# Two gate projections as stages of seven block products, attention on two tracks, and the first branch's values in blocks of 512 columns

## The chip, the core and the metric

One core of a Trainium2 chip runs the whole program. Its engines work side by side and wait for each other through semaphores: TensorE (PE in the profile, its weight loads PEld) multiplies matrices into PSUM, VectorE (DVE) and ScalarE (ACT) do elementwise work, GpSimd (POOL) does some adds and issues DMAs, and SyncE (SP) issues most loads. The metric is device time in microseconds (us) of one execution; a comparison uses the median of several.

## The reference

One layer of a decoder trunk on x (1024 x 1024, float32). One combined projection feeds two mixers that run in parallel on the same input: HGRN2 (8 heads of 128) and gated linear attention (GLA, 4 heads with 128 key and 256 value columns). Each has a SiLU gate z, each is projected, and sigmoid gates merge them:

```python
proj = h @ w_in[l]                                   # h: modulated RMS norm of x
hq, hf, hi, hz, gq, gk, gv, gz, ga, mg = jnp.split(proj, IN_OFFSETS, axis=-1)
y_h = rms_norm(linear_attention(silu(hq), k, hi, log_f, 1.0), hgrn_norm_w) * silu(hz)
y_g = rms_norm(linear_attention(gq, gk, gv, log_a, K ** -0.5), gla_norm_w) * silu(gz)
u_h, u_g = y_h @ w_branch[l, 0], y_g @ w_branch[l, 1]
mg = sigmoid(mg.reshape(B, T, 2, D))
merged = mg[:, :, 0] * u_h + mg[:, :, 1] * u_g
x = x + gate[:, None, :] * (merged @ w_out[l])
return rms_norm(x, final_norm_w)
```

The HGRN norm goes over all 1024 columns, the GLA norm over one head's 256. The attention is computed by chunks of 64 steps.

## The kernel before

Every float32 product is made of three matmuls on operands split in a high and a low part (`split`, L195 for the low part on DVE): high times high, high times low, low times high. Activations lie transposed, channels on partitions, 1024 steps along the free side.

The program has four parts. **The beginning** loads x, makes the modulation and the transposed normalised input `h_hi`, `h_lo`, and the first projections. **The stream** (`Stream.go`) runs a list of jobs: `Feat` projects 128 columns (48 matmuls of 512 columns, L454), `Vblk` makes one GLA head's 256 value columns (192 matmuls of 256 columns, L513 to L515), `Vblk2` makes 512 value columns for four HGRN heads (192 matmuls of 512 columns, L556 to L558). After every unit of a job (six matmuls of 512 columns, or twelve of 256) `weave` lets two tracks advance by a count of units: `side`, the attention of one head after another, and `back`, which prepares factors and weights for the last part. **The stages** (`last_stages`, `Pair.run`, L1313) are large products in a block form with seven products of half size in place of eight (`PRODUCTS`): a stage has 7 products x 4 pairs of column blocks x 12 matmuls = 336. Before, there are four: the two merge gates from h (stages 0 and 1, sharing the factors `H` of h), and the two branch projections (2 and 3). Their factors are sums of quadrants of the activations; their weights are raw quadrants or sums of quadrants. The sums of weights are made early by `weight_sums` (two loads, four adds on DVE, four stores to `w_sums` in DRAM) and fetched again by `load_duo`; `prep_duo` splits them (L1256), `build` splits the factors (L1234). **The end** (`OutBlk`) is the output projection and the last norm.

`attention` (L570 on) has a first half that builds a head's masked scores in `scT` with many small DVE steps, and a second half that makes the states and the outputs and calls `post`. `post` multiplies the output by the norm weight and by the gate, which `silu_done` (L865, L866) had made from a z projection; the result is stored to `yg_d` or `yh_d`. Only one attention runs at a time on `side`. The last one reaches into stage 0: `scores_done` and `side_done` wait for it there before its PSUM banks are lent to the stages. The norm of the HGRN branch, `rst_h`, is known when its last head is done, and `scale_quad` (L1212) applies it when stage 3's quadrants have been loaded.

The order in which an engine's instructions stand is set by a scheduler from these calls and a planner's costs; each engine then runs strictly in that order, and so does the queue of loads on SP. Tiles of 4 KB per partition come from 46 slots (`Slots`), and `ahead` loads and splits weights while enough of them are free.

Of the kernel before, what the change touches and what calls it, by code (L numbers as in the profile page):

```python
# [15 lines left out]
P = 128  # L16
# [66 lines left out]
def hybrid_trunk_kernel(  # L83
# [346 lines left out]
    scoring = set()  # L430
# [48 lines left out]
    class Vblk:  # L479

        raws, parts = 2, 4

        def __init__(self, col, done):
            self.col, self.done = col, done

        def load(self):
            self.raw = []
            for kk in range(2):
                b = S.get([4, 256])
                nc.sync.dma_start(b, w_in2[kk * 512:(kk + 1) * 512, self.col:self.col + 256].rearrange(  # L490
                    "(k p) f -> p k f", p=P))
                self.raw.append(b)

        def prep(self):
            self.wt = []
            for b in self.raw:
                hi = S.get([4, 256], F32R)
                lo = S.get([4, 256], F32R)
                split(b, hi, lo)
                self.wt.append((hi, lo))  # L500
                S.free(b)

        def run(self):
            v = [S.get([4, 256]) for _ in range(2)]
            for g in range(2):
                ps = dtile()
                for i in range(4):
                    t = g * 4 + i
                    for k in range(KT):
                        hi, lo = self.wt[k // 4]  # L510
                        lh, ll = h_hi[k][:, t * P:(t + 1) * P], h_lo[k][:, t * P:(t + 1) * P]
                        o = ps[:, i * 256:(i + 1) * 256]
                        nc.tensor.matmul(o, lh, hi[:, k % 4, :], start=(k == 0), stop=False)  # L513
                        nc.tensor.matmul(o, lh, lo[:, k % 4, :], start=False, stop=False)  # L514
                        nc.tensor.matmul(o, ll, hi[:, k % 4, :], start=False, stop=(k == KT - 1))  # L515
                        if k % 4 == 3:
                            yield
                nc.scalar.copy(v[g].rearrange("p a b -> p (a b)"), ps)
            for hi, lo in self.wt:
                S.free(hi, lo)  # L520
            self.done(v)

    class Vblk2:

        raws, parts = 4, 8
# [18 lines left out]
        def run(self):  # L544
            v = [S.get([2, 512]) for _ in range(4)]
            for g in range(4):
                if g == 2:
                    self.middle()
# [992 lines left out]
```

## Time and profile before

| what | value |
|---|---|
| median of 3 runs | 1251.07 us (1250.69 to 1251.1) |
| the profiled execution | 1252.38 us |
| its span, first to last instruction | 1250.7 us |
| granted PE clock, mean | 0.99 |
| stream (L454 first and last start) | 127.9 to 825.3 us |
| stages (L1313 first and last start) | 825.5 to 1154.0 us |
| last weight sum stored (L1171) | 606.9 us |

A row of the groups by line reads: line, engine, operation, output and inputs, shape, count, then busy us and mean ns of one, then how long the engine stood idle before such an instruction and what ended it. Busy time counts stretches in which two instructions overlap once. A row by stretches reads: start and end, length, then busy us and count for PE, PEld, DVE, ACT and POOL, then granted clock, DMA share and GB/s.

### The profile page before, as it was taken

The page shows a single profiled execution, that of the slowest core. Times are in us where ns is not written, and L with a number is a line of the kernel's source. Part 1 is how long each engine was busy: PE and PEld are TensorE (multiplying, and loading weights), DVE is VectorE, ACT ScalarE, POOL GpSimd, SP SyncE. Part 2 cuts the span into 40 slices and gives each one's busy share as a digit, 9 for nine tenths or more (in the row PEclk, how much of TensorE's full clock was granted, in tenths as well). Part 3 has the DMA queues.
Part 4 walks back from the last instruction along what each step waited for, and adds up shares of the span by engine and source line. Part 5 has one row for each costly group of instructions (what it writes and reads, how often), then busy time and mean ns, then how long its engine had stood idle before and what let it go on. Part 6 is the DMA issues. An engine that isn't in the chain of part 4 may idle for free.

```text
span 1250.7 us, 20782 instructions
## 1 busy us (share of the span) xinstructions
PE 1205.7 (96%) x8603; PEld 999.9 (80%) x8603; DVE 765.2 (61%) x1219; ACT 530.4 (42%) x784; POOL 132.4 (11%) x216
## 2 busy tenths in 40 slices
PE   4799999999999999999999999999999999998997
PEld 3676899989798888788887878877888888787786
DVE  5746425494857556777873365695422668979443
ACT  4467713343334344243332323456643644454222
POOL 5510000201211021021110101011110000000000
PEclk9899999999999999999999999999999999999999
DMA  8832100653644167255251212154546556235202
GB/s 269 278 115 86 52 18 18 217 188 102 203 143 144 63 208 254 92 179 174 96 177 45 60 41 68 38 183 169 173 163 225 179 171 201 83 100 170 118 34 101
DMA packets 126928, 168.82 MB, mean 135 GB/s; under 512 B 7019, under 2 KB 97185, under 8 KB 126834
## 3 DMA queue, kind: packets, MB, share of 16 engines
q1 hardware_dynamic: 115234, 129.53, 33.5%
q0 software_dynamic: 11552, 37.97, 7.8%
q8 instruction: 67, 1.10, 0.4%
q14 instruction: 27, 0.22, 0.1%
q10 hardware_dynamic: 48, 0.01, 0.0%
HBM read 125.53 MB, written 41.94 MB: 134 GB/s over the span
## 4 chain that ended last, share of the span: by engine, by line
PE 59%; issue 24%; DVE 8%; DMA 3%; POOL 2%; ACT 2%; SPq 1%; POOLq 0%; DVEq 0%; ACTq 0%
PE pd L454 13%; PE pd L1313 11%; PE sc_ps L1313 5%; PE pm L1313 5%; PE pd L556 2%; PE pd L557 2%; PE pd L558 2%; DVE scT L250 1%; PE pm L761 1%; PE pm L742 1%; PE pm L763 1%; PE pd L1083 1%; PE pd L1084 1%; PE pd L1085 1%; DVE b L195 1%
## 5 line engine op out<-in xcount | busy, mean ns | idle before, releaser
L454 PE MATMUL pd<-b,b 128*128 128x512 f32 x1632 | 386.3, 393 | 0.0
L454 PEld LDWEIGHTS pd<-b,b 128*128 128x128 f32 x1632 | 302.4, 188 | 64.0 <-issue 0.5
L1313 PE MATMUL pd<-b,b 128*128 128x512 f32 x720 | 175.7, 395 | 2.5 <-DVE b L866 1.5
L1313 PEld LDWEIGHTS pd<-b,b 128*128 128x128 f32 x720 | 134.7, 189 | 35.4 <-DVE b L866 1.9
L195 DVE TENSOR_TENSOR b<-b,b 128x1024 fp32r<-128x1024 f32 (+1 forms) x95 | 101.8, 1082 | 74.7 <-ACT b L192 34.8
L192 ACT CAST b<-b 128x1024 fp32r<-128x1024 f32 (+1 forms) x95 | 84.6, 904 | 104.0 <-DVE b L1169 14.7
L1256 DVE TENSOR_TENSOR b<-b,b 128x1024 fp32r<-128x1024 f32 x56 | 68.3, 1224 | 68.5 <-ACT b L1255 46.6
L1255 ACT CAST b<-b 128x1024 fp32r<-128x1024 f32 x56 | 58.5, 1051 | 62.8 <-PE pd L1313 17.2
L1313 PE MATMUL sc_ps<-b,b 128*128 128x512 f32 x324 | 79.0, 391 | 0.3 <-ACT scT L706 0.3
L1313 PE MATMUL pm<-b,b 128*128 128x512 f32 x300 | 72.5, 389 | 3.4 <-DVE b L1256 3.4
L513 PE MATMUL pd<-b,b 128*128 128x256 f32 x256 | 74.2, 290 | 0.0
L515 PE MATMUL pd<-b,b 128*128 128x256 f32 x256 | 72.5, 283 | 0.0
L514 PE MATMUL pd<-b,b 128*128 128x256 f32 x256 | 72.4, 283 | 0.0
L1313 PEld LDWEIGHTS sc_ps<-b,b 128*128 128x128 f32 x324 | 60.4, 188 | 13.6 <-ACT scT L706 0.8
L1313 PEld LDWEIGHTS pm<-b,b 128*128 128x128 f32 x300 | 56.3, 188 | 15.5 <-DVE b L1256 3.8
L1234 DVE TENSOR_TENSOR b<-b,b 128x1024 fp32r<-128x1024 f32 x36 | 45.1, 1263 | 18.1 <-ACT b L1233 10.3
L1171 POOL DMA_DIRECT2D ws<-b x64 | 34.6, 541 | 194.8 <-DVE b L1165 87.1
L556 PE MATMUL pd<-b,b 128*128 128x512 f32 x128 | 52.0, 406 | 0.0
L557 PE MATMUL pd<-b,b 128*128 128x512 f32 x128 | 50.4, 394 | 0.0
L558 PE MATMUL pd<-b,b 128*128 128x512 f32 x128 | 50.4, 394 | 0.0
L648 ACT COPY xb<-b 128x512 f32<-128x512 f32 x48 | 29.5, 620 | 49.3 <-PE sc_ps L628 26.3
L1233 ACT CAST b<-b 128x1024 fp32r<-128x1024 f32 x36 | 37.2, 1049 | 28.9 <-PE pd L1313 10.1
(268 smaller groups left out, 2041.9 us busy)
## 6 DMA issues: line engine op xcount, KB each, us to landing
b<-in_w_in_dram SPq DMA_DIRECT2D x66, 512.0 KB, 4.0
ws<-b POOLq DMA_DIRECT2D x64, 256.0 KB, 3.0
b<-ws SPq DMA_DIRECT2D x32, 512.0 KB, 4.2
b<-in_x_dram SPq DMA_DIRECT2D x16, 512.0 KB, 5.8
b<-in_ada_w_dram SPq DMA_DIRECT2D x32, 256.0 KB, 6.2
b<-in_w_branch_dram SPq DMA_DIRECT2D x16, 512.0 KB, 4.8
b<-h SPq DMA_DIRECT2D x14, 512.0 KB, 4.2
b<-in_w_in_dram SPq DMA_DIRECT2D x24, 256.0 KB, 3.5
```

Source lines behind the costliest of these rows:

```text
L192: i = nc.scalar.copy(hi, src)
L195: (eng or nc.vector).tensor_sub(lo, src, hi.bitcast(F32))
L454: nc.tensor.matmul(ps[0:w, th * 512:(th + 1) * 512], a[:, k, 0:w], b[:, th * 512:(th + 1) * 512], start=(k == 0 and n == 0), stop=(k == KT ...
L513: nc.tensor.matmul(o, lh, hi[:, k % 4, :], start=(k == 0), stop=False)
L514: nc.tensor.matmul(o, lh, lo[:, k % 4, :], start=False, stop=False)
L515: nc.tensor.matmul(o, ll, hi[:, k % 4, :], start=False, stop=(k == KT - 1))
L556: nc.tensor.matmul(o, lh, hi[:, k % 2, :], start=(k == 0), stop=False)
L557: nc.tensor.matmul(o, lh, lo[:, k % 2, :], start=False, stop=False)
L558: nc.tensor.matmul(o, ll, hi[:, k % 2, :], start=False, stop=(k == KT - 1))
L1255: nc.scalar.copy(hi, t)
L1256: nc.vector.tensor_sub(lo, t, hi.bitcast(F32))
L1313: nc.tensor.matmul(o, a[:, sl], c, start=(p in (1, 5) and kt == 0 and n == 0), stop=(kt == 3 and n == 2), skip_group_check=True)
```

## The change

The z projections leave the stream. Two stages more, from the same factors of h, make them: the order is now merge gate 1, GLA's z, HGRN's z, merge gate 0, branch 1, branch 0, six stages in all, and the factors of h stay in their slots through four of them. `attention` stores y without the gate (`post` only copies with the norm weight, on ACT). In the z stages `load_y` fetches y again, `put_z` takes the silu on ACT, multiplies on DVE (for HGRN by the root `rst_h` too) and stores the result. `scale_quad` is gone. `weight_sums` makes 24 groups where it made 16.

`attention` is cut in `scores` and `outputs`, and `Stream` has a track `out` more: outputs of one head may run while the next head's scores are made, until these would overwrite `scT` (`reading`). `Vblk` is gone; two `Vblk2` make the values of two GLA heads each. `side_done` alone waits for both tracks, in stage 0 after the third pair of its fourth product, and then lends the banks, after one dummy matmul in each half of `sc_ps`. The gate vector of the residual (`gate_side`) moves to the preparing track behind the second stage's weight sums. The free slots that `ahead` demands rise, and sums and differences on the preparing track keep their place in program order.

```diff
-    class Vblk:
-        raws, parts = 2, 4
...
@@ attention @@
-        scoring.discard(me)
-        yield 3.5
+        reading[0] += 1
+        return cur
+
+    def outputs(q, k, cur, v, vo, V, post):
...
+        while reading[0]:
+            yield 1
...
-            yield 3
+            if vh < nvh - 1:
+                yield 3
+        reading[0] -= 1
         S.free(q, *st)
+        yield 3
@@ Stream @@
+            self.out = deque()
...
-                if d > loads or d > 0 and room() < job.raws + 4:
+                if d > loads or d > 0 and room() < job.raws + 8:
...
-                if d > preps or d > 0 and room() < job.parts + 1:
+                if d > preps or d > 0 and room() < job.parts + 5:
...
-            for track, pace in ((self.side, PACE), (self.back, 1)):
+            for track, pace in ((self.out, self.pace), (self.side, self.pace), (self.back, 1)):
@@ gla_attention, post @@
-                g[vh] = qk.pop(("z", h, vh))
-                sq[vh] = S.get([T])
+                g[vh], sq[vh] = S.get([T]), S.get([T])
             sl = slice(half * 512, half * 512 + 512)
             nc.scalar.activation(sq[vh][:, sl], po, AF.Square)
-            nc.vector.scalar_tensor_tensor(g[vh][:, sl], po, vec[:, R_GN + vh:R_GN + vh + 1],
-                                           g[vh][:, sl], ALU.mult, ALU.mult)
+            nc.scalar.activation(g[vh][:, sl], po, AF.Copy, scale=vec[:, R_GN + vh:R_GN + vh + 1])
...
-    for h in range(4):
-        if h >= 2:
-            J.append(Feat(col(C_GK + h * P), rhs_h, gla_k_done(h)))
-        J.append(Feat(col(C_GZ + h * 256), rhs_h, silu_done(g_state, ("z", h, 0))))
-        J.append(Feat(col(C_GZ + h * 256 + P), rhs_h, silu_done(g_state, ("z", h, 1))))
+    for h in (0, 2):
+        if h:
+            J.append(Feat(col(C_GK + 2 * P), rhs_h, gla_k_done(2)))
+            J.append(Feat(col(C_GK + 3 * P), rhs_h, gla_k_done(3)))
...
-        J.append(Vblk(C_GV + h * 256, v_done))
+        def v_half(h=h):
+            start_side(gla_attention(h), 3)
+            start_side(gla_attention(h + 1))
+        J.append(Vblk2(C_GV + h * 256, v_done, v_half))
...
-        J.append(Feat(col(C_HZ + h * P), rhs_h, silu_done(h_state, ("z", h))))
...
-    sources = [[col(C_MG + n * D + d * P, 2 * P) for d in range(0, 8, 2)] for n in (1, 0)]
+    sources = [[col(c0 + d * P, 2 * P) for d in range(0, 8, 2)] for c0 in (C_MG + D, C_GZ, C_HZ, C_MG)]
...
-        while len(S.free_list) < 12:
+        while len(S.free_list) < (10 if b < 4 else 7):
...
-        for b in range(4):
+        for b in range(6):
             for i in range(4):
                 yield from weight_sums(b, i)
+            if b == 1:
+                yield from gate_side()
...
-    def scale_quad(b, z):
...
+    def load_y(acts, d, half):
+        y_half[d, half] = Q.get()
+        nc.sync.dma_start(y_half[d, half], part_y(acts, d, half))
+
+    def put_z(acts, scaled):
+        def put(d, half, ap, summed):
+            g = ap if summed else Q.get()
+            y = y_half.pop((d, half))
+            nc.scalar.activation(g, ap, AF.Silu)
+            if scaled:
+                nc.vector.tensor_mul(y, y, rst_h[0][:, half * 512:half * 512 + 512])
+            nc.vector.tensor_mul(g, g, y)
+            nc.gpsimd.dma_start(part_y(acts, d, half), g)
+            Q.free(g, y)
+        return put
...
-    outs[:] = [put_gate1, put_gate0, put_t1, put_m]
+    outs[:] = [put_gate1, put_z(yg_d, False), put_z(yh_d, True), put_gate0, put_t1, put_m]
...
     def side_done():
-        while stream.side:
+        while stream.side or stream.out:
             stream.weave(1)
+        for z in (sc_ps[:, 0:512], sc_ps[:, 512:1024]):
+            nc.tensor.matmul(z, ones_r, H[0, 1][0][0].rearrange("p a t -> p (a t)")[:, 0:512], start=True, stop=True,
+                             skip_group_check=True)
+            R.lend([z])
         R.lend([mtile(), mtile()])
-        for i in (2, 3):
+        for i in range(4):
             pairs[0, i].seed()
-    after(0, 2, 3, scores_done)
...
+    after(0, 3, 2, side_done)
...
+    stream.pace = 1.15
```

What the scheduler makes of it is shown at three places. The first is PE, in the first block of values of the GLA branch, before (b_1156 and its neighbours are the weights, b_140 and on are parts of h):

```order
L513 MATMUL pd_1193<-b_1156,b_147 128x256
L514 MATMUL pd_1193<-b_1157,b_147 128x256
L515 MATMUL pd_1193<-b_1156,b_155 128x256
L513 MATMUL pd_1193<-b_1152,b_140 128x256
L514 MATMUL pd_1193<-b_1153,b_140 128x256
```

and now:

```order
L513 MATMUL pd_1086<-b_1081,b_147 128x512
L514 MATMUL pd_1086<-b_1082,b_147 128x512
L515 MATMUL pd_1086<-b_1081,b_155 128x512
L513 MATMUL pd_1086<-b_1069,b_140 128x512
L514 MATMUL pd_1086<-b_1070,b_140 128x512
```

The sequence is the same, each instruction has twice the columns, and there are half as many.

The second place is DVE where the attention of the last head but one meets the splits for stage 0 (L656, L657, L698 are steps of the scores, L1256 a weight split, L1234 a factor split, L746 and L748 states, L991 the forget gate of the last head). Before:

```order
L656 TENSOR_TENSOR b_6913<-b_6913,tot_775 128x8x64
L657 TENSOR_TENSOR b_6803<-b_6803,tot_775 128x8x64
L698 COPY_PREDICATED blk<-mask_767,sc_ps 128x8x16
L1256 TENSOR_TENSOR b_7383<-b_7156,b_7382 128x1024
L1234 TENSOR_TENSOR b_7488<-b_7379,b_7486 128x1024
L746 COPY b_7278<-pm_7279 128x128
L748 SCALAR_TENSOR_TENSOR b_7278<-b_7278,tot_775,pm_7279 128x128 x3
L748 SCALAR_TENSOR_TENSOR b_7278<-b_7278,tot_775,pm_7288 128x128 x3
L991 TENSOR_SCALAR b_7307<-b_7307,oml,lb 128x1024
```

Now (L610, L611, L654 are the steps of the scores, L1134 the adds of `weight_sums`, L1221 a weight split, L958 the forget gate):

```order
L611 TENSOR_TENSOR b_5435<-b_5435,tot_775 128x16x32
L613 TENSOR_TENSOR tot_775<-tot_775 128x16
L1134 TENSOR_TENSOR b_5934<-b_5787,b_5788 128x512
L1134 TENSOR_TENSOR b_5934<-b_5935,b_5788 128x512
L613 TENSOR_TENSOR tot_775<-tot_775 128x8
L1221 TENSOR_TENSOR b_6042<-b_5653,b_6041 128x1024
L1134 TENSOR_TENSOR b_5935<-b_5934,b_5788 128x512
L1221 TENSOR_TENSOR b_6102<-b_5928,b_6101 128x1024
L958 TENSOR_SCALAR b_6032<-b_6032,oml,lb 128x1024
L610 TENSOR_TENSOR b_5633<-b_5633,tot_775 128x8x64
L611 TENSOR_TENSOR b_5435<-b_5435,tot_775 128x8x64
L654 COPY_PREDICATED blk<-mask_767,sc_ps 128x8x16
```

Adds of weight sums now stand among the scores and the splits. Behind the first factor split of stage 0 stand 40 of 96 of them; before, none of 64.

The third place is DVE between the last two stages (L1398 and L1384 multiply by a merge gate, L1212 is the scaling of quadrants, L1234 and L1199 factor splits, L1256 and L1221 weight splits). Before:

```order
L1398 TENSOR_TENSOR b_8910<-b_8910,pd_7419 128x512
L1234 TENSOR_TENSOR b_9242<-b_9035,b_9240 128x1024
L1256 TENSOR_TENSOR b_9261<-b_9180,b_9260 128x1024
L1398 TENSOR_TENSOR b_8925<-b_8925,pm_7939 128x512
L1212 TENSOR_TENSOR b_9130<-b_9130,b_7883 128x1024
L1212 TENSOR_TENSOR b_9199<-b_9199,b_7883 128x1024
L1398 TENSOR_TENSOR b_8947<-b_8947,pd_7419 128x512
L1212 TENSOR_TENSOR b_9200<-b_9200,b_7883 128x1024
```

and now:

```order
L1384 TENSOR_TENSOR b_8780<-b_8780,pd_6039 128x512
L1221 TENSOR_TENSOR b_9127<-b_9050,b_9126 128x1024
L1384 TENSOR_TENSOR b_8795<-b_8795,pd_6040 128x512
L1199 TENSOR_TENSOR b_9181<-b_8954,b_9179 128x1024
L1199 TENSOR_TENSOR b_9182<-b_8955,b_9180 128x1024
L1384 TENSOR_TENSOR b_8817<-b_8817,pm_6688 128x512
```

The eight scalings are no longer there.

More of the change, by code (lines that the diff above doesn't have):

```diff
@@ L544, in run @@
         def run(self):
[L545 removed]
+            v = []
             for g in range(4):
+                v.append(S.get([2, 512]))
                 if g == 2:
@@ L883, in gla_attention, with gla_outputs @@
         qk = g_state
-        v = qk.pop(("v", h))
+        q, k = qk.pop(("q", h)), qk.pop(("k", h))
+        cur = yield from scores(q, k, alphas[h])
+        stream.out.append([gla_outputs(h, q, k, cur), 3.5])
+    def gla_outputs(h, q, k, cur):
+        qk = g_state
         g = {}
@@ L902, in gla_attention @@
         inverse_root(rst, sq[0], 256)
-        for half in range(4):
-            sl = slice(half * 256, half * 256 + 256)
-            for vh in range(2):
-                nc.vector.tensor_mul(g[vh][:, sl], g[vh][:, sl], rst[:, sl])
-            yield 1.5
+        for vh in range(2):
+            nc.vector.tensor_mul(g[vh], g[vh], rst)
+            yield 1
         for vh in range(2):
@@ L999, in hgrn_attention, with hgrn_outputs @@
         st = h_state
+        q, k = st.pop(("q", h)), st.pop(("k", h))
+        cur = yield from scores(q, k, st.pop(("f", h)))
+        stream.out.append([hgrn_outputs(h, q, k, cur), 3.5])
+    def hgrn_outputs(h, q, k, cur):
+        st = h_state
         y = [None]
```

143 lines of the change are left out of this document (49 added, 94 removed).

## The prediction

> **What bounds the kernel now.** I read the page's busy table first, then the chain that ended last, then busy time by stretches.
>
> ```profile
> span 1250.7 us, 20782 instructions
> PE 1205.7 (96%) x8603; PEld 999.9 (80%) x8603; DVE 765.2 (61%) x1219; ACT 530.4 (42%) x784; POOL 132.4 (11%) x216
> PE 59%; issue 24%; DVE 8%; DMA 3%; POOL 2%; ACT 2%; SPq 1%; POOLq 0%; DVEq 0%; ACTq 0%
> ```
>
> TensorE (PE) is busy 96% of the span and VectorE (DVE), the next, 61%; the chain lies on PE for 59% and for 24% in issue, where the profile shows no wait at all. A busy PE need not be a fast one, so the rate has to be checked. The view by stretches gives, for each, its length, then busy time and instruction count by engine, then PE clock, DMA share and GB/s.
>
> ```profile
> 75.00:825.00 750.00, 743.36 (x6368) 625.43 (x6368) 461.78 (x818) 304.14 (x442) 83.05 (x116) 1.00 0.37 119
> 825.00:901.00 76.00, 73.49 (x562) 58.74 (x561) 47.45 (x70) 49.39 (x72) 7.90 (x11) 1.00 0.50 163
> 901.00:977.00 76.00, 76.00 (x336) 62.80 (x335) 25.30 (x25) 32.23 (x44) 4.31 (x8) 1.00 0.62 205
> 977.00:1053.00 76.00, 76.00 (x337) 62.92 (x337) 50.71 (x51) 35.73 (x44) 0.00 (x0) 1.00 0.53 166
> ```
>
> The first row is the stream of projections with the attention woven in, the others are about the first three block-product stages. The third is a clean gate stage: 336 matmuls in 76.0 us, 0.2262 us each, at the full granted clock, and nobody waited for. The chain of waits shows the same pace in the stream (L454) and in a stage (L1313), start and length of twelve 512-column matmuls:
>
> ```profile
> 687.71 2.72 PE pd L454 x12
> 950.47 2.72 PE sc_ps L1313 x12
> ```
>
> 2.72 / 12 = 0.2267 us. So PE runs at its own rate nearly everywhere after the start: in the stream it idled 750 - 743.36 = 6.6 us. Matmuls taken out come off the end, as long as the rest still hides.
>
> The Trainium skill, "Perfetto Trace Analysis", section Identifying the Most-Contended Engine, says that matmul busy time is a poor measure of headroom, and that the busy share of weight loads should be used. By that PE would have 20% to spare here (80%), and taking matmuls away would bring little. The clean stage disagrees: weight loads are busy 62.80 of 76 us there, 83%, with PE never idle, so about 83% is a full PE in this shape.
>
> **Gate projections become stages.** Removed: sixteen `Feat` jobs (eight z blocks of each branch), 48 matmuls each, 768 x 0.2267 = 174.1 us. Added: two stages of 336, 672 x 0.2267 = 152.3 us. Difference **-21.8 us**. The Trainium skill, "TensorE: Matmul & The Clock Gate", section Back-to-back issue gap, gives about 131 ns for a sustained 512-column matmul; by it these 96 would bring 12.6 us. The rows here say 226 to 227 ns.
>
> **Values of the first branch.** `Vblk` ran 768 matmuls of 256 columns. The timeline (start, length) shows their pace:
>
> ```profile
> 155.23 0.28 PE L513 MATMUL pd<-b,b 128*128 128x256 f32 x1
> 156.31 0.28 PE L513 MATMUL pd<-b,b 128*128 128x256 f32 x1
> ```
>
> Nine steps in 1.08 us, 0.120 us each: 92.2 us. Two `Vblk2` run 384 of 512 columns, 87.1 us: **-5.1 us**. Half the columns cost 0.120 and not 0.113, that is all the gain. Two dummy matmuls in `side_done` add 0.5. PE in sum: -21.8 - 5.1 + 0.5 = **-26.4 us**.
>
> **What the new stages hang on DVE, ScalarE (ACT) and the queues.** Means from the groups by line:
>
> ```profile
> L195 DVE TENSOR_TENSOR b<-b,b 128x1024 fp32r<-128x1024 f32 x63 | 79.0, 1258 | 65.6 <-ACT b L192 25.8 <-PE pd L515 19.3 <-DMA yh<-b 6.5
> L1256 DVE TENSOR_TENSOR b<-b,b 128x1024 fp32r<-128x1024 f32 x56 | 68.3, 1224 | 68.5 <-ACT b L1255 46.6 <-DMA gate<-b 5.6 <-PE pm L720 3.6
> L866 DVE TENSOR_TENSOR b<-b,pd 128x1024 f32<-128x1024 f32 x24 | 29.4, 1223 | 12.4 <-ACT b L865 12.4
> L1405 DVE TENSOR_TENSOR b<-b,b 128x512 f32<-128x512 f32 x8 | 5.5, 686 | 0.0
> L1212 DVE TENSOR_TENSOR b<-b,b 128x1024 f32<-128x1024 f32 x8 | 9.7, 1222 | 6.9 <-DMA b<-yh 6.9
> L894 DVE SCALAR_TENSOR_TENSOR b<-pm,vec,b 128x512 f32<-128x512 f32 x16 | 12.0, 751 | 40.7 <-ACT b L893 40.7
> L1383 ACT ACTIVATE b<-b 128x512 f32<-128x512 f32 x8 | 5.0, 630 | 4.3 <-DVE b L1300 4.3
> ```
>
> A gate stage for z has the weight splits and sums of the clean one plus, per half row, a silu (0.63 on ACT), a product with y (0.686 on DVE), and for the second branch one more product. That is 16 x 0.686 = 11 us of DVE for the first branch and 22 for the second: 25.3 becomes 36 and 47 of 76 us, ACT 32.2 becomes 42. Both hide behind PE's 76. The loads and stores of y are 32 pieces of 256 KB, 8.4 MB in a stage or 110 GB/s; with fourteen 512 KB weight tiles (97 GB/s) that is the 205 GB/s of the clean row, where PE waited for no one. POOL gets 64 more DMA issues on 132 us busy, 0.54 us each:
>
> ```profile
> L1171 POOL DMA_DIRECT2D ws<-b x64 | 34.6, 541 | 194.8 <-DVE b L1165 87.1 <-DVE b L1166 54.1 <-DVE b L748 15.8
> ```
>
> All of this I cost at nothing; without the cover, the second branch's 47 us of DVE would be what counts first.
>
> **Where DVE is no longer cover: stage 0.** The preparing track now sums 24 weight groups and not 16. In the order of DVE, 40 of its 96 adds stand behind the first factor split of stage 0; before, none of 64 did.
>
> ```profile
> L1165 DVE TENSOR_TENSOR b<-b 128x512 f32<-128x512 f32 x16 | 11.0, 690 | 9.4 <-PE pm L761 4.3 <-PE pd L454 2.7 <-DMA b<-in_w_in_dram 1.9
> L1166 DVE TENSOR_TENSOR b<-b,b 128x512 f32<-128x512 f32 x16 | 12.7, 792 | 18.6 <-DMA b<-in_w_branch_dram 4.9 <-DMA yg<-b 3.3 <-PE sc_ps L596 3.3
> L1168 DVE TENSOR_TENSOR b<-b,b 128x512 f32<-128x512 f32 x16 | 12.6, 788 | 0.1
> L1169 DVE TENSOR_TENSOR b<-b,b 128x512 f32<-128x512 f32 x16 | 11.0, 687 | 0.2
> ```
>
> Four adds are 2.96 us, ten groups 29.6. Stage 0 had 47.45 us of DVE in 76 with the last heads in it; less the last head's two products of 0.75, which go to ACT as copies, it becomes 47.5 + 29.6 - 1.5 = 76 of 76. Behind each add wait the splits of stage 0's factors and weights, which PE needs next, and the attention of the last two heads. What a full DVE costs PE is read from the stretches in which it was full:
>
> ```profile
> 250.00:275.00 25.00, 23.61 (x285) 19.31 (x275) 23.95 (x46) 10.42 (x20) 2.14 (x4) 1.00 0.73 236
> 325.00:350.00 25.00, 23.59 (x275) 19.26 (x274) 24.13 (x50) 12.08 (x21) 2.16 (x4) 1.00 0.42 131
> 550.00:575.00 25.00, 24.76 (x227) 20.11 (x227) 24.78 (x48) 8.00 (x12) 6.64 (x11) 1.00 0.67 220
> 1050.00:1075.00 25.00, 24.84 (x108) 19.84 (x108) 25.00 (x29) 13.03 (x14) 0.00 (x0) 1.00 0.57 173
> 1125.00:1150.00 25.00, 21.54 (x87) 16.97 (x86) 25.00 (x37) 13.35 (x17) 0.00 (x0) 0.93 0.42 135
> ```
>
> PE lost 1.39, 1.41, 0.24, 0.16 and 3.46 us in them, 1.33 on average. Three such slices: **+4.0 us**, from 0.5 (three of the cheapest) to 10.4 (three of the dearest). I take the mean, since stage 0 mixes heads, as the first three slices do, with splits, as the last two do.
>
> **The denser stream.** Attention stays and the projections around it shrink. DVE loses sixteen splits (20.1), sixteen silu products (19.6), the 32 products behind the heads (0.75 each, 24) and two of the sixteen weight groups (5.9): 461.8 - 69.6 = 392 us, in 750 - 179.2 = 571, or 69% where it was 62%. The two tracks put one head's scores beside another's outputs; three heads' outputs at most can be late for it, because the scores wait in `reading`. I add one more slice like 325 to 350: **+1.4 us**, from -1 (sixteen fewer waits of PE for an evacuation) to +7 (the 6.6 us lost there once more).
>
> **The end.** Eight products with the root, 9.7 us (L1212), leave the full DVE near 1050 to 1075. What PE lost at 1125 to 1150 lies 50 us later, so only part of the backlog can have lasted: **-1.0 us**, from -4.1 (3.46 there and 0.64 in the slice behind it) to 0.
>
> ```profile
> 1150.00:1175.00 25.00, 24.36 (x107) 19.65 (x106) 18.16 (x24) 7.83 (x13) 0.00 (x0) 1.00 0.64 232
> ```
>
> **Sum.** -26.4 + 4.0 + 1.4 - 1.0 = -22.0 us. The profiled execution took 1252.38 us, its span 1250.7; the median of the runs is 1251.07. So 1230.4 for a profiled execution, and **1229 us** as the time.
>
> **Rivals.** *Nothing stalls.* The adds fall into gaps of DVE and the end drains: -26.4 - 4.1 = -30.5, 1221 us. For it speaks that two of the full slices cost PE 0.2 us or less; against it, that stage 0 leaves no gap. *DVE sets the pace* in stage 0 and among the heads: 10.4 + 7 instead of the 5.4, and no gain at the end, -9.0, 1242 us. For it speaks the slice at 1125; against it, that PE had work in store in the other four. *Loads come late.* SP issues 72 more loads in one order, and one that waits for its buffer holds those behind it. The waits of SP's queue (total, times, longest):
>
> ```profile
> SPq L436 <- PE pd L454: 66.4, 6, 25.4
> SPq L1200 <- PE pd L454: 49.8, 4, 31.7
> ```
>
> A weight tile is loaded two products ahead, 96 x 0.2267 = 21.8 us. If such a wait of 31.7 us stood ahead of the tiles at a stage's beginning, PE would lose 9.9 us; from the third such entry on the change loses, and at all four from stage 1 to 4 it gives 1251.1 - 22.0 + 39.6 = 1269 us, slower than before. Against it: the longest waits all lie in the stream, and the clean stage, whose loads share the queue with the quadrants, shows none that PE felt.
>
> **Chances.** The forecast 0.60, nothing stalls 0.15, DVE sets the pace 0.18, late loads 0.05; 0.02 is left for a mix that ends near the old time. This kernel's measurements can tell 0.2%, 2.5 us, from no change. So faster 0.93, same 0.02, slower 0.05. The range takes in the forecast's own 1224 to 1236, and reaches to the first two rivals: 1219 to 1243.
>
> **What would show it.** Right: 864 matmuls at L454's successor and 2016 in the stages, stages 1 to 3 with 336 in about 76 us each and PE never idle; DVE above 95% in stage 0 and PE idle there for 3 to 6 us, released by DVE splits. The stream should end about 179 us earlier. Wrong: PE idle at the beginning of stages 1 to 4, released by DMA or by splits behind a DMA; y products that hold a bank so that the next product waits; or a score matmul that waits for ScalarE's copies in every head.

## The result, and the profile after

The changed kernel takes 1293.61 us (median, 1290.98 to 1297.45), the kernel before 1250.88 in the same runs: ratio 1.0345, 95% interval 1.0325 to 1.0366. It is slower, and lies above the range of 1219 to 1243.

The page of the changed kernel, first the lines that answer to those of before, then the granted clock in 40 slices of 32 us:

```profile
span 1291.7 us, 20303 instructions
PE 1198.9 (93%) x8125; PEld 979.1 (76%) x8125; DVE 783.8 (61%) x1247; ACT 573.0 (44%) x866; POOL 172.0 (13%) x280
PEclk9799999999998999999998988998999999999999
PE 41%; DMA 7%; issue 5%; DVE 3%; ACT 2%; POOL 1%; SPq 0%; POOLq 0%; ACTq 0%; DVEq 0%
```

PE has 478 matmuls fewer, yet it is busy only 6.8 us less (1205.7 before) and idle 92.8 us where it was idle 45.0. In the chain DMA has grown from 3% to 7%, and "issue", PE waiting for nobody, has fallen from 24% to 5%.

The view by stretches, cut at the ends of the stages, shows where. Columns as in the prediction: length, busy time and count of PE, PEld, DVE, ACT, POOL, then clock, DMA share, GB/s. First the kernel before (stream, stages 0 to 3, end):

```profile
75.00:825.50 750.50, 743.86 (x6371) 625.81 (x6371) 462.25 (x819) 304.52 (x443) 83.05 (x116) 1.00 0.37 119
825.50:917.80 92.30, 89.79 (x634) 72.11 (x633) 53.68 (x76) 55.52 (x81) 11.67 (x18) 1.00 0.53 171
917.80:994.00 76.20, 76.20 (x338) 63.12 (x337) 31.51 (x31) 35.54 (x48) 0.54 (x1) 1.00 0.60 194
994.00:1070.90 76.90, 76.74 (x337) 62.94 (x337) 55.70 (x59) 34.31 (x40) 0.00 (x0) 1.00 0.53 164
1070.90:1154.00 83.10, 79.33 (x337) 63.30 (x336) 74.10 (x90) 39.77 (x51) 0.00 (x0) 0.98 0.36 117
1154.00:1250.70 96.70, 88.44 (x385) 71.43 (x383) 44.31 (x74) 26.05 (x55) 0.00 (x0) 0.97 0.24 90
```

Then the changed kernel (stream, stages 0 to 5, end):

```profile
75.00:666.70 591.70, 564.69 (x5168) 461.30 (x5167) 380.66 (x705) 276.30 (x419) 79.94 (x107) 0.98 0.40 129
666.70:795.10 128.40, 106.68 (x685) 85.92 (x684) 81.93 (x125) 62.89 (x100) 30.14 (x49) 0.89 0.74 246
795.10:871.80 76.70, 76.70 (x339) 63.48 (x339) 35.34 (x45) 32.03 (x44) 12.99 (x24) 1.00 0.76 255
871.80:960.80 89.00, 80.39 (x338) 65.53 (x338) 43.96 (x55) 30.45 (x42) 9.76 (x18) 0.94 0.58 192
960.80:1041.80 81.00, 77.46 (x337) 62.30 (x336) 32.50 (x32) 37.07 (x50) 0.54 (x1) 1.00 0.55 175
1041.80:1117.90 76.10, 76.10 (x337) 63.06 (x336) 52.37 (x56) 33.36 (x39) 0.00 (x0) 1.00 0.55 174
1117.90:1197.50 79.60, 77.39 (x339) 63.20 (x339) 66.32 (x82) 39.93 (x52) 0.00 (x0) 1.00 0.36 119
1197.50:1291.70 94.20, 86.60 (x383) 71.39 (x381) 46.41 (x77) 26.23 (x55) 0.00 (x0) 0.97 0.26 95
```

Against the forecast for each part (before, with the prediction's terms put in):

| part | forecast | measured | difference |
|---|---|---|---|
| stream ends at | 825.5 - 179.2 + 1.4 = 647.7 | 666.7 | +19.0 |
| stage 0 | 92.3 + 4.0 + 0.5 = 96.8 | 128.4 | +31.6 |
| stage 1 (GLA's z) | 76.2 | 76.7 | +0.5 |
| stage 2 (HGRN's z) | 76.2 | 89.0 | +12.8 |
| stage 3 (merge gate 0) | 76.2 | 81.0 | +4.8 |
| stage 4 | 76.9 | 76.1 | -0.8 |
| stage 5 and end | 83.1 + 96.7 - 1.0 = 178.8 | 173.8 | -5.0 |

The differences add up to 62.9, and the span is 1291.7 - 1228.7 = 63.0 us above its forecast. Stage 1, with a second trip of y, sixteen products more and 255 GB/s, is as clean as forecast. The losses lie in the stream, in stage 0 and around stage 2, and nowhere there is DVE full: 64% of the stream and of stage 0, half of stage 2. Lengths of stages here and below are those of one profiled execution of each kernel.

What a loss looks like is read at the beginning of stage 2. PE's timeline (start, length, in brackets the idle time ahead and what ended it):

```profile
883.57 4.74 PE L1278 MATMUL pd<-b,b 128*128 128x512 f32 x12 [6.35 <-ACT pd L1261]
888.15 2.88 PE L1278 MATMUL pm<-b,b 128*128 128x512 f32 x12
```

ACT's:

```profile
876.29 0.60 ACT L1365 ACTIVATE b<-sc_ps 128x512 f32<-128x512 f32 x1 [4.82 <-issue]
881.98 1.05 ACT L1220 CAST b<-b 128x1024 fp32r<-128x1024 f32 x1 [5.09 <-DMA yg<-b]
882.93 0.58 ACT L1261 ACTIVATE pd<-pd 128x512 f32<-128x512 f32 x1
```

SP's, with the cast's own load:

```profile
869.72 0.93 SPq L1213 DMA_DIRECT2D b<-in_w_in_dram  x2
```

And the chain that ended last, at the same place:

```profile
876.50 5.46 DMA yg<-b
881.98 0.02 ACT b L1220
882.93 0.59 ACT pd L1261
```

PE waits 6.35 us for the seed of a bank (L1261). ACT could have made it when the product was done, but ahead of it in ACT's order stands the cast of a weight tile (L1220), which waits 5.09 us. It does not wait for its tile: by the semaphores in the trace its two loads, which left SP at 869.72, had landed by 875.2. What ended the wait is the landing of a store of y (`yg<-b`), issued at 876.50. The cast needs no data from it; the natural reading is that it writes into the slot that the store still reads. So a slot that comes back late reaches PE through an evacuation that has nothing to do with it. Then PE needs 4.74 us for twelve matmuls where the next twelve take 2.88, at a granted clock of 0.50 from 883.6 to 887.2. In stage 0, at 680, a factor's cast stands in the evacuation's way, and it too waits for the landing of a store, here of a weight sum:

```profile
675.07 1.04 ACT L1198 CAST b<-b 128x1024 fp32r<-128x1024 f32 x1 [8.22 <-DMA ws<-b]
676.02 1.06 ACT L659 COPY scT<-sc_ps 32x128 f32<-32x128 f32 x4
677.09 0.75 ACT L662 COPY scT<-sc_ps 64x256 f32<-64x256 f32 x2
677.74 1.64 ACT L665 COPY scT<-blk 32x256 f32<-32x256 f32 x4
679.41 0.60 ACT L1252 ACTIVATE b<-pd 128x512 f32<-128x512 f32 x1
```

and PE behind it:

```profile
680.06 5.49 PE L1278 MATMUL pd<-b,b 128*128 128x512 f32 x12 [6.29 <-ACT b L1252]
```

Elsewhere it is a load that is late, because it waited for such a slot itself. For the gap of 4.14 us at 710.86 the chain reads:

```profile
697.35 6.92 DMA ws<-b
704.33 4.91 DMA b<-h
709.26 0.02 ACT b L1195
```

Eleven gaps after 130 us are longer than 2 us. Behind five of them (401.83, 680.06, 710.86, 762.80 and 883.57) stands an evacuation behind a cast, and the chain leads back to the landing of a store: the cast waits for it directly at 680 and 883, in the other three its load did. Of the rest, four end with a late step on VectorE.

The gap itself is two thirds of the price. Summed over stretches of 10 us, PE's busy time times what is missing of the clock is 31.5 us, before 9.3. The longer idle time (47.8) and the slower clock (22.2) together are 70 us, against about 29 us of work taken out (1205.7 - 9.3 less 1198.9 - 31.5): 41 us, the growth of the span.

### The profile page after: what moved, and what is told of

It reads as the page before. It is cut to its first block, busy times and chain, and to the rows that moved or that the text cites. A ratio compares the mean times of both kernels' runs of the same rounds, so it can differ in the third digit from the quotient of the medians.

```text
span 1291.7 us, 20303 instructions
## 1 busy us (share of the span) xinstructions
PE 1198.9 (93%) x8125; PEld 979.1 (76%) x8125; DVE 783.8 (61%) x1247; ACT 573.0 (44%) x866; POOL 172.0 (13%) x280
## 4 chain that ended last, share of the span: by engine, by line
PE 41%; DMA 7%; issue 5%; DVE 3%; ACT 2%; POOL 1%; SPq 0%; POOLq 0%; ACTq 0%; DVEq 0%
PE pd L1278 13%; PE pm L1278 7%; PE sc_ps L1278 5%; PE pd L454 3%; DMA b<-in_w_in_dram 2%; DMA yg<-b 1%; PE pd L1053 1%; PE pd L1051 1%; PE pd L1052 1%; DMA b<-yh 1%; PE pd L513 1%; PE pd L514 1%; PE pd L515 1%; DMA ws<-b 1%; ACT b L1220 1%
## 5 line engine op out<-in xcount | busy, mean ns | idle before, releaser
L1278 PE MATMUL pd<-b,b 128*128 128x512 f32 x1056 | 260.9, 401 | 26.4 <-ACT b L1252 6.5
L1278 PEld LDWEIGHTS pd<-b,b 128*128 128x128 f32 x1056 | 201.9, 193 | 73.4 <-ACT b L1252 7.1
L454 PE MATMUL pd<-b,b 128*128 128x512 f32 x864 | 210.1, 397 | 0.0
L454 PEld LDWEIGHTS pd<-b,b 128*128 128x128 f32 x864 | 160.5, 189 | 34.4 <-issue 0.2
L1221 DVE TENSOR_TENSOR b<-b,b 128x1024 fp32r<-128x1024 f32 x84 | 102.3, 1222 | 112.6 <-ACT b L1220 75.9
L1220 ACT CAST b<-b 128x1024 fp32r<-128x1024 f32 x84 | 87.3, 1051 | 111.5 <-PE pd L1278 15.4
L195 DVE TENSOR_TENSOR b<-b,b 128x1024 fp32r<-128x1024 f32 (+1 forms) x79 | 81.3, 1042 | 74.9 <-ACT b L192 56.8
L1278 PE MATMUL sc_ps<-b,b 128*128 128x512 f32 x456 | 115.6, 404 | 8.8 <-ACT b L1252 4.9
L1278 PE MATMUL pm<-b,b 128*128 128x512 f32 x504 | 120.8, 389 | 0.0
L1278 PEld LDWEIGHTS sc_ps<-b,b 128*128 128x128 f32 x456 | 89.1, 196 | 29.8 <-ACT b L1252 5.5
L1278 PEld LDWEIGHTS pm<-b,b 128*128 128x128 f32 x504 | 94.7, 188 | 19.7
L513 PE MATMUL pd<-b,b 128*128 128x512 f32 x256 | 104.6, 408 | 0.0
L514 PE MATMUL pd<-b,b 128*128 128x512 f32 x256 | 100.3, 392 | 0.0
L515 PE MATMUL pd<-b,b 128*128 128x512 f32 x256 | 100.2, 392 | 0.0
L1141 POOL DMA_DIRECT2D ws<-b x96 | 52.0, 542 | 254.4 <-DVE b L1134 193.2
L1199 DVE TENSOR_TENSOR b<-b,b 128x1024 fp32r<-128x1024 f32 x36 | 44.2, 1244 | 27.8 <-ACT b L1198 17.6
L513 PEld LDWEIGHTS pd<-b,b 128*128 128x128 f32 x256 | 48.6, 190 | 11.7 <-issue 1.2
L515 PEld LDWEIGHTS pd<-b,b 128*128 128x128 f32 x256 | 48.3, 189 | 10.6
L514 PEld LDWEIGHTS pd<-b,b 128*128 128x128 f32 x256 | 48.6, 190 | 9.9 <-issue 0.5
L1198 ACT CAST b<-b 128x1024 fp32r<-128x1024 f32 x36 | 37.6, 1052 | 40.8 <-PE pd L1278 9.0
```

Source lines behind the costliest of these rows:

```text
L195: (eng or nc.vector).tensor_sub(lo, src, hi.bitcast(F32))
L454: nc.tensor.matmul(ps[0:w, th * 512:(th + 1) * 512], a[:, k, 0:w], b[:, th * 512:(th + 1) * 512], start=(k == 0 and n == 0), stop=(k == KT ...
L513: nc.tensor.matmul(o, lh, hi[:, k % 2, :], start=(k == 0), stop=False)
L514: nc.tensor.matmul(o, lh, lo[:, k % 2, :], start=False, stop=False)
L515: nc.tensor.matmul(o, ll, hi[:, k % 2, :], start=False, stop=(k == KT - 1))
L1141: nc.gpsimd.dma_start(w_sums[b][i // 2][q][:, i % 2 * 512:i % 2 * 512 + 512], parts[p].rearrange("p k f -> p (k f)"))
```

## The experiments

Ratios are against the kernel before, run beside each. Edits are against the changed kernel where nothing else is said.

**Who issues the loads.** In the first run the sums' loads, in the second the loads of y go out from GpSimd:

```diff
-            nc.sync.dma_start(x.rearrange("p k a f -> p k (a f)"),
+            nc.gpsimd.dma_start(x.rearrange("p k a f -> p k (a f)"),
```

> The 48 loads of the weight sums (L1128) are issued from GpSimd's queue in place of SyncE's; nothing else is changed. Theory A (order of the loads: a weight or factor load stands on SP behind a weight-sum load that waits for its slot, the cast for it stands on ScalarE, and PE waits for an evacuation behind that cast): the 8.4 us gap near 402, the 6.3 us near 680 and the 4 to 5 us near 711, 763 and 790 go or halve, 15 to 30 us in all with the slow clock behind them, so 1263 to 1279 us. Theory B (the DMA engines are full in stage 0, share 0.74 on average and up to 0.96, and every load lands late whatever queue issues it): 1290 to 1297, no change.

```diff
-        nc.sync.dma_start(y_half[d, half], part_y(acts, d, half))
+        nc.gpsimd.dma_start(y_half[d, half], part_y(acts, d, half))
```

> The changed kernel with the 32 loads of y (L1359) issued from GpSimd's queue and not from SP's; all else is the same. Leaving y out gained 16.7 us. If that was the order of SP's queue (a load of y waits for its half slot and holds the weight loads behind it): 1277 to 1284 us. If it was the slots that y takes, or its traffic: 1289 to 1297.

Measured: 1293.13 us (1.0347, 1.032 to 1.0374) and 1298.61 us (1.0389, 1.0357 to 1.042). Neither helps; theory A, in the form that one load holds others behind it, falls. The second run shows what holds in its place. The waits of SP's queue at the beginning of stage 2 (what waits, for what; total, times, longest), first in the changed kernel:

```profile
SPq L1359 <- DMA yg<-b: 13.5, 5, 5.2
```

and with y's loads on GpSimd:

```profile
SPq L1213 <- DVE b L1368: 13.2, 1, 13.2
SPq L1209 <- DMA yg<-b: 9.7, 1, 9.7
```

In the changed kernel loads of y do stand there for stores of y, ahead of the weight tiles. With no load of y in the queue, a weight tile itself waits 9.7 us for a store of y. It needs no data from it; it waits for its slot. PE's gap stayed, 6.03 us, and the cast ahead of the seed again waited for a store of y. The Trainium skill, "DMA: Bandwidth & Descriptors", section Issuing engines are not separate DMA queues, says that spreading DMAs over engines saves no more than the time to issue them; both runs agree.

**Leaving work out.** First the last eight groups of weight sums, then y's second trip:

```diff
-        for b in range(6):
+        for b in range(4):
...
-            nc.sync.dma_start(t.rearrange("p a f -> p (a f)"), w_sums[b][j][SUMS[p]])
+            nc.sync.dma_start(t.rearrange("p a f -> p (a f)"), w_sums[b % 4][j][SUMS[p]])
```

> The last eight groups of weight sums (both branches) are not made, and the branch stages fetch the sums of the first two groups of stages instead, so that the branch products are computed with other weights; 16 of the 48 loads and 32 of the 96 stores of the sums are left out, some 16 MB, and 32 adds. Theories A and B both expect stage 0 to shrink from 128 us towards its 108 us of PE work: 1263 to 1278 in all. If the third theory holds (C: attention on two tracks makes PE wait for the score steps), stage 0 keeps its gaps: above 1285. The gap near 402 lies before these groups and should stay under A and B.

```diff
-        y_half[d, half] = Q.get()
-        nc.sync.dma_start(y_half[d, half], part_y(acts, d, half))
+        pass
...
-            nc.vector.tensor_mul(g, g, y)
-            nc.gpsimd.dma_start(part_y(acts, d, half), g)
-            Q.free(g, y)
+            Q.free(g)
```

> The changed kernel without the meeting of z and y: y is not fetched, multiplied or stored again in stages 1 and 2, so the branches get y without its gate; silu is still taken. 64 transfers of 256 KB, 48 products on VectorE and the half slots of y are left out. If the slots and the queue's order around y cause the losses of stage 2 (12.8 us over a clean stage) and of the beginning of stage 3 (4.8): 1274 to 1280. If they come from elsewhere: 1288 to 1296.

Measured: 1282.63 us (1.0264, 1.0245 to 1.0283) and 1276.91 us (1.0216, 1.0197 to 1.0235). The first lies between the ranges (1263 to 1278, above 1285) and decides for no theory; the second lies in the range for the slots and the queue's order around y. Without the sums, stage 0 and stage 2:

```profile
662.50:781.90 119.40, 103.07 (x687) 84.19 (x686) 67.52 (x102) 63.95 (x101) 18.42 (x27) 0.92 0.51 170
858.20:946.60 88.40, 79.56 (x337) 64.53 (x336) 43.71 (x55) 30.66 (x43) 9.17 (x17) 0.96 0.58 189
```

Without y, stages 0, 2 and 3:

```profile
665.80:794.60 128.80, 108.48 (x688) 87.19 (x687) 82.90 (x126) 64.04 (x101) 30.61 (x51) 0.87 0.74 246
871.00:947.40 76.40, 76.40 (x339) 63.25 (x338) 22.58 (x22) 31.04 (x43) 0.00 (x0) 1.00 0.34 103
947.40:1026.10 78.70, 77.64 (x339) 62.84 (x338) 30.25 (x30) 36.56 (x49) 0.00 (x0) 1.00 0.51 161
```

Without the sums stage 0 is 9.0 us shorter, and the stream 4.2; without y stage 2 is 12.6 shorter, with PE never idle, and stage 3 2.3. In the twelve runs that have both z stages and y's second trip, stage 2 takes 85 us or more, so its 12.6 belong to y; stage 3 takes 77 to 84 in them, which leaves its 2.3 open. That DMA was less busy without the sums (0.51 against 0.74) and two thirds of stage 0's loss were still there speaks against theory B.

**The late sums elsewhere.**

```diff
+    def late_sums():
+        for b in (4, 5):
+            for i in range(4):
+                yield from weight_sums(b, i)
...
+    after(3, 1, 0, lambda: stream.back.append([late_sums(), 1]))
```

> The changed kernel with the sums of the branch weights (the last 8 of 24 groups) made from the second product of stage 3 on, where no y is fetched, instead of in stage 0 and 1. The run without these groups was 11 us faster than the changed kernel; if their place was what cost and not their work, this gets the same: 1280 to 1286 us. If the work costs the same anywhere: 1290 to 1296.

Measured: 1291.71 us (1.0327, 1.0297 to 1.0356). Stage 0 shrank from 128.4 to 120.4 us; stage 2 grew by 1.6, ahead of the moved sums, stage 3 by 2.8 to 83.8 and stage 4 by 2.5 to 78.6. The time lies in the range for work that costs the same anywhere.

**Order and engine of what waits.**

```diff
-            tc.keep_in_program_order(nc.vector.tensor_add(*ops))
+            nc.vector.tensor_add(*ops)
```

> The sums, the differences of the factors and the gate vector's steps no longer keep their place in program order, so that the scheduler may put them elsewhere among VectorE's instructions. If the kept places are what makes VectorE stand for late loads (theory K), the score gaps near 373, 610 and 665 (2.6, 3.1 and 3.2 us) go and the time falls by 8 us or more, to 1285 or less. By theory A the loads are as late as before, another instruction stands for them: 1285 to 1300.

```diff
-        nc.scalar.copy(hi, t)
+        nc.gpsimd.tensor_copy(hi, t)
```

> The high parts of the stages' weights and factors (L1220, L1195, L1198) are cast on GpSimd instead of ScalarE, so that a late load no longer stands in ScalarE's order ahead of the evacuations. Theory A: the gaps of the stages that end with ScalarE (6.3, 4.9, 4.5, 4.1, 6.4 us and the slow clock behind each) go, unless PE then lacks the weights themselves: 1255 to 1275. If the loads are so late that PE needs their weights at that moment, the gaps stay, ended by VectorE's splits instead: 1285 to 1300. Both suppose that GpSimd makes a cast of 128 x 1024 in less than 5 us.

Measured: 1294.62 us (1.035, 1.0297 to 1.0404) and 1300.57 us (1.0405, 1.0384 to 1.0426). Kept places are no cause of the total. But stage 0 changes with them, though no work is gone, by as much as it did without the sums:

```profile
669.60:789.30 119.70, 103.74 (x689) 83.18 (x686) 80.06 (x123) 65.94 (x103) 31.03 (x51) 0.93 0.77 258
```

Stage 0 is 8.7 us shorter, stage 1 3.2 longer (79.9). So the 9.0 us of the run without the sums do not show that the sums cost them. With the casts on GpSimd, PE's gaps ended by ACT near 680 and 711 were gone and the one at 883 fell to 2.87 us, but others came: 5.99 us near 718 for a DVE step of the scores, 5.02 near 779 and 5.94 near 1135 for casts on GpSimd. The one near 718 leads back to a late load, which has found another engine to stand on. The one near 1135 does not: there two casts with a change of sign (L1195), 2.85 us each on the mean, begin when a product ends. So the run trades one loss for another.

**Parts of the change alone.** On the kernel before: the values by `Vblk2`, then the two tracks.

```diff
-        J.append(Vblk(C_GV + h * 256, v_done))
+        J.append(Vblk2(C_GV + h * 256, v_done, v_half))
```

> The kernel before with one part of the change alone: GLA's values as two Vblk2 of 512 columns. By the prediction's term PE has 5.1 us less to do and the rest hides: 1246 us. If 1 MB more of weights at once, or two heads started from one job, make loads late, it gives that back: 1251 or more.

```diff
-            for track, pace in ((self.side, PACE), (self.back, 1)):
+            for track, pace in ((self.out, PACE), (self.side, PACE), (self.back, 1)):
```

> The kernel before with another part alone: attention cut into scores and outputs on two tracks. It takes no work from PE. Theory C (two tracks make PE wait for score steps and copies): 1258 us or more. Theory D (the sixteen z projections were what covered late loads and heads in the stream; without them the same loads are wanted in 590 instead of 750 us): 1247 to 1253, no change.

Measured: 1252.91 us (1.0028, 1.0008 to 1.0049) and 1272.87 us (1.0181, 1.0152 to 1.0211). The values bring no 5.1 us: PE's busy time falls by 2.9 (1202.8) and its idle time grows by 2.2 (1250.0 - 1202.8 = 47.2). The tracks seemed to be the cause. So the changed kernel got one track again, at two paces:

```diff
-PACE = 1.1
+PACE = 1.4
...
-        stream.out.append([hgrn_outputs(h, q, k, cur), 3.5])
+        yield 3.5
+        yield from hgrn_outputs(h, q, k, cur)
```

> The changed kernel with one track again: a head's outputs follow its own scores before the next head's scores begin, and the pace is 1.4 in place of 1.1 so that twelve heads fit into the shorter stream. Two tracks alone cost the kernel before 1.8%, 22.6 us. If they cost the same here (theory C): 1265 to 1275 us. If the stalls come from the thinner cover of the stream whatever the tracks (theory D): 1285 to 1300.

> The same with the pace at 1.25: the attention is spread further and more of it is left for stage 0. Theory C: within 6 us of the run with 1.4, to either side. If what counts is how much attention is left in stage 0, it is 5 us or more above that run.

Measured: 1299.22 us (1.0398, 1.0376 to 1.042) and 1301.04 us (1.041, 1.0389 to 1.043). In the changed kernel one track is no better, at either pace. That speaks against theory C there, though the pace was changed with the track, and the pace alone moved 14 us (last run below).

**HGRN's z back in the stream**, with two tracks and with one:

```diff
+        J.append(Feat(col(C_HZ + h * P), rhs_h, silu_done(h_state, ("z", h))))
...
-    outs[:] = [put_gate1, put_z(yg_d, False), put_z(yh_d, True), put_gate0, put_t1, put_m]
+    outs[:] = [put_gate1, put_z(yg_d, False), put_gate0, put_t1, put_m]
```

> The changed kernel with HGRN's z back in the stream as eight projections and only GLA's z as a stage (five stages, 20 groups of weight sums). PE's sum against before is 48 matmuls (10.9 us) less for the stage and 5.1 less for the values: 1235 us if nothing stalls. Theory D: most stalls of the second half of the stream and of stage 0 go with the cover back, 1238 to 1252. If the stages' own traffic is the cause (sums of weights, y fetched again), about half of the 64 us stays: 1260 or more.

> HGRN's z in the stream, only GLA's z as a stage, and one track at a pace of 1.25. With two tracks this came to 1265 us, 30 above its sum. If C and D together are the cause, it comes to 1238 to 1247, faster than the kernel before; if the tracks are not the cause here, 1260 to 1270.

Measured: 1265.15 us (1.0117, 1.0091 to 1.0144) and 1262.98 us (1.0106, 1.0084 to 1.0129). Both lie where the stages' own traffic (1260 or more) and "not the tracks" (1260 to 1270) had them, and theory D's 1238 to 1252 did not come. Still, more than half of the stalls go: with both z as stages the time stands 69 us above PE's sum of 1224.7 (1251.1 - 26.4), with one 30 above 1235. Stage 0 is 95.3 us. But the stream alone is 22 us over its sum (755.1 against 825.5 - 87.1 - 5.1 = 733.3), with either number of tracks. The stage behind GLA's z, which now is a merge gate without any y, shows where that branch's second trip is paid. Stage 1 (GLA's z) and the stage behind it:

```profile
850.40:926.70 76.30, 76.30 (x339) 63.16 (x338) 28.79 (x34) 31.34 (x43) 7.56 (x14) 1.00 0.57 188
926.70:1010.60 83.90, 78.61 (x339) 64.21 (x338) 35.53 (x36) 37.07 (x49) 1.62 (x3) 0.98 0.58 188
```

The stage itself is clean, and the one behind it loses 7.7 us.

**Cover put back.** Sixteen projections that nobody reads, in the stream:

```diff
+        J.append(Feat(col(C_HZ + h * P), rhs_h, lambda ps: None))
```

> The changed kernel with sixteen projections put back in the stream at about their old places, whose products nobody reads (the stages still make z): work added, output unchanged. PE gets 768 x 0.2267 = 174.1 us more. Theory D (the projections were the cover in which late loads, heads and sums caught up): most stalls of the stream and of stage 0, about 45 us with the slow clock, go, 1415 to 1435 us. If cover is not the cause: 1462 to 1472.

Measured: 1431.55 us (1.1455, 1.1427 to 1.1483), 137.9 more for 174.1 us of work: 36.2 come back. Stages 0, 2 and 3:

```profile
830.00:932.70 102.70, 92.80 (x571) 74.45 (x570) 48.73 (x72) 54.95 (x80) 11.47 (x18) 0.95 0.50 163
1009.00:1098.20 89.20, 81.02 (x338) 66.00 (x338) 43.65 (x55) 30.25 (x42) 9.56 (x18) 0.94 0.57 191
1098.20:1179.60 81.40, 77.78 (x339) 62.71 (x338) 32.47 (x32) 37.69 (x50) 0.70 (x2) 1.00 0.51 174
```

25.7 of them come from stage 0, where now one head's outputs lie and not two (16 matmuls of L718 in place of 32) and no weight sum (the last add starts at 658.7, ahead of the stage); 10.8 come from the stream (830.0 against 666.7 + 174.1), although it also does the head's outputs that stage 0 no longer has. The time lies in theory D's range. Stages 2 and 3 lose what they lost.

**Neighbours.** One slot less, in the changed kernel and in the one before, two less in the one before, and another pace in the changed one:

```diff
-N_SLOTS = 46
+N_SLOTS = 45
```

> The changed kernel with 45 slots in place of 46. Theory S (slots are what binds: each load waits for the last reader of a slot given back a moment ago): 6 us slower or more, above 1299. If slots are not scarce: 1288 to 1297.

> The kernel before with 45 slots, to compare with the last one: theory S expects it to lose less than half as much as the changed kernel does, 1249 to 1253 us.

> The kernel before with 44 slots. With 45 it lost 1.5%, 19 us, while the changed kernel gained 12 with one slot less, so scarcity is not what one slot changes. Theory T (the kernel before is a tuned point: any other assignment of slots costs some 20 us, and the changed kernel stands at an ordinary one): 1260 to 1285 us. If slots are simply scarce in the kernel before, it loses as much again: 1285 or more.

```diff
-PACE = 1.1
+PACE = 1.2
```

> The changed kernel with a pace of 1.2 in place of 1.1 for both tracks, another neighbour of it that takes no work away. Theory T: anywhere from 1270 to 1305 us, as with 45 slots. Whatever it is, by the structural losses shown (y's second trip, the thin cover) it should stay above 1262.

Measured: 1281.22 us (1.0242, 1.0205 to 1.028), 1268.51 us (1.0152, 1.0123 to 1.0182), 1247.9 us (0.9989, 0.9976 to 1.0003) and 1279.44 us (1.0248, 1.0221 to 1.0274). Theory S falls, since the changed kernel gains by having one slot less; so does theory T in its strong form, since the kernel before loses nothing with two less. What stays is a spread: an edit that takes no work away moved these kernels by 1 to 20 us. Differences of that size between kernels that are arranged differently prove nothing by the total time. That holds nearly for the two tracks on the kernel before (23 us) and for the small changes in the other runs. Single stages spread too: stage 0 by 8.7 us without a change of work, and stage 1, 76.7 in the changed kernel, is some 84 with one slot less. What is left clear of it are stage 2 with and without y, and the 36.2 us of the cover. No run is clearly below the kernel before.

## Why the prediction was wrong

**PE's sum, -26.4: held.** 864 matmuls at L454 and 2016 at L1278 are there, and about 29 us of work are gone. The share of the values (-5.1) brought no time alone.

**"All of this I cost at nothing": the step that failed, for both branches.** I priced the loads and stores of y by GB/s and by VectorE's products, and both do hide: stage 1 took 76.7. VectorE's 36 and 47 us came out at 35.3 and 44.0; ScalarE's 42 was too much (32.0 and 30.5), since the silu stands where the clean stage had its sigmoid. What I did not price is the half slot of y, which comes back when its store has landed, after silu, product, issue and transfer. The casts and loads of the next stage's weight tiles wait for such slots. Shown: 12.6 us of stage 2 go with y, and the wait for the store outlives the move of y's loads. That the slot is what is waited for, and not y's traffic, is read from the traces and was not tried by itself.

The first branch's trip costs its own stage nothing and the stage behind it the most. Its last three stores of y are issued after stage 1 has ended at 871.8 (874.76 to 881.15), and the gap of 6.35 us with its 1.86 of slow clock lies behind one of them; in the run with GLA's z as the only such stage, the stage behind loses 7.7 us. The second branch's part of stage 2 is another gap:

```profile
941.94 0.69 DVE L1367 TENSOR_TENSOR b<-b,b 128x512 f32<-128x512 f32 x1 [2.37 <-DMA b<-yh]
945.03 4.61 PE L1278 MATMUL sc_ps<-b,b 128*128 128x512 f32 x12 [2.27 <-DVE b L1265]
```

VectorE stands for a load of y with the product by the root (L1367), and the evacuation L1265 behind it comes late: 2.27 us idle and 1.73 of slow clock. Together the two gaps are 12.2 of the stage's 12.8 us.

**Stage 0, +4.0 for a full VectorE: wrong mechanism and size.** DVE is busy 64% of the stage. I had seen that 40 adds move into it and counted their time, not that sums, two heads and the stage's own tiles recycle the same slots: SP stands there for stores and readers of slots, as its waits from 640 to 795 show:

```profile
SPq L1213 <- PE pd L454: 25.1, 1, 25.1
SPq L1172 <- DMA ws<-b: 14.9, 7, 6.4
SPq L1213 <- DMA ws<-b: 13.5, 2, 12.8
SPq L1209 <- DVE b L705: 13.3, 1, 13.3
```

Of the 31.6 us some 9 are the second head's matmuls, only moved there (L677, L699, L718 and L720 are busy 16.8 us in the stage, the same lines 8.2 before). The rest, some 23, no run divides: 9.0 go without the late sums, but 8.7 go as well when only the order on VectorE changes. With the cover put back 25.7 of the 31.6 go, the head's included.

**The denser stream, +1.4: measured +19.0,** or about 28 with the head that it passed on. The z projections were not only work; they were the time in which heads and sums finished. Putting that time back recovered 36.2 us, in stream and stage 0, more than any edit without work moved. How much of the stream's rest is the thin cover and how much the arrangement stays open: 22 us are lost too with HGRN's z back, and one slot less takes 14 us off the changed kernel's stream (652.6).

**The end, -1.0: measured -6.0;** they became shorter by more than the bound of -4.1.

**The clock was in no term.** 22.2 us of the miss are matmuls at a slower clock, about half of the full one behind each of PE's gaps shown here. The Trainium skill, "TensorE: Matmul & The Clock Gate", section HAM oscillation, asks for no idle gap above about 3.4 us. Here 2.27 us were enough once (twelve matmuls in 4.61 us at 945.03, 2.88 without a gap), and 2.59 us at 373.38 were not.

**The rival "Loads come late"** came nearest and got a chance of 0.05. Its reason, a wait that holds the loads behind it, was not it: taking the sums' or y's loads out of the queue brought no time. What holds the tiles is the store that still has their slot. Its price (9.9 at each entry of stages 1 to 4) fits one entry, stage 2's, 6.35 idle and 1.86 of slow clock; most of the loss lies in the stream and in stage 0. I set it low because the clean stage of before showed no such wait, but hardly a store gave slots back there (one DMA issue on POOL, 0.54 us, in stage 1 of before; 18, 9.76 us, in stage 2 now). The count alone does not say it: stage 1 now has 24 and is clean.

**"DVE sets the pace" and "nothing stalls"** are both refuted by the 64% and by the gaps.

## What to carry to other kernels

Work that is removed from a stream also removes the time behind which everything else finishes; ask of each late task when it will now end, and what it shares with the next stage. A buffer that leaves by a store is free when the store has landed, so price a trip through DRAM by the wait for its buffer and not by bytes. Before a small difference is put down to an edit, measure a neighbour that differs in arrangement alone, and read the effect from the stage that it should touch, if that stage stays put among the neighbours. When an instruction waits, read what ended the wait before blaming its own load: here it was a store that still had the buffer.

## What the runs showed of the hardware

A gap on PE costs more than its length: 6.35 us idle were followed by twelve matmuls in 4.74 us instead of 2.88, 6.29 us by twelve in 5.49, 2.27 us by twelve in 4.61. A cast of 128 x 1024 to the matmul's format takes 1.25 us on GpSimd, 1.05 on ScalarE:

```profile
L1220 POOL CAST b<-b 128x1024 fp32r<-128x1024 f32 x84 | 104.0, 1248 | 160.0 <-DVE b L1221 24.2 <-PE sc_ps L1278 21.1 <-DMA b<-ws 20.0
```
